# HGRN values of seven heads turned through memory and VectorE instead of TensorE, and the decode steps moved behind the heads' decode products, in a hybrid HGRN2 / Mamba-2 layer

## The chip, the cores and the metric

The kernel runs on one core of one Trainium2 chip. The metric is the device time of one launch, in microseconds. A core has five engines that take their instructions in order and wait for each other by semaphores: TensorE (PE in the profile, with its weight loads as PEld), VectorE (DVE), ScalarE (ACT), GpSimd (POOL) and SyncE (SP). In this kernel nearly all DMAs are issued by SP, in the order in which they stand in its queue; an issue that has to wait for something holds back every issue behind it.

## The reference

One decoder layer is computed for two groups of tokens: a prompt of 1024 tokens, and eight single tokens (decode) that bring recurrent states of their own. Per layer:

```
proj = rmsnorm(x) @ w_in                      # 1024 -> q, f, i, g, z, xbc, dt
# group A, HGRN2, 8 heads of 128 x 128
f = lb + (1-lb)*sigmoid(f_r);  k = 1-f;  q = silu(q_r);  v = i_r
S_t = f_t * S_(t-1) + k_t v_t^T;   o_t = q_t S_t        # chunks of 64
o_a = rmsnorm(o) * silu(g)
# group B, Mamba-2, 16 heads of 64, state 128
xbc = silu(conv(xbc));  h_t = exp(A dt_t) h_(t-1) + dt_t x_t B_t^T;  y_t = C_t h_t + D x_t
y = rmsnorm(y * silu(z))
x = x + concat(o_a, y) @ w_out
x = x + (silu(conv(gate)) * val) @ w_down      # gate, val = rmsnorm(x) @ w_up
```

After a final RMSNorm the two outputs and all new states are returned: among them the HGRN states of the prompt (`hgrn_prompt`) and of the eight decode tokens (`hgrn_sample`), and the SSM states of the decode tokens (`ssm_sample`).

## The kernel before, in words

Activations lie with the feature on the 128 partitions and the 1032 tokens (T = 1024 prompt tokens, then ND = 8 decode tokens, NT in all) along the free dimension. A matrix product of full precision is made of three products of halves (`hh` by `wh`, `hl` by `wh`, `hh` by `wl`): a weight tile `ws` comes from memory by DMA (512 KB), ACT rounds it to `wh` (L199), DVE makes the remainder `wl` (L201), and TensorE runs 72 matmuls over three column blocks of 344 tokens. One such job yields one of the arrays `f`, `q`, `v`, `sg` of one HGRN head, which ACT evicts from PSUM in three pieces (L924).

The program has, in order, the input projection and the SSM part (to about 370 us), eight HGRN heads (372.6 to about 870 us), and the output projection with the MLP. `head(h, t)` is a generator of small PE steps (score products `a`, state products `od` and `kv`, outputs `o`) with DVE, ACT and POOL work between them. TensorE's order is written out: `drive` interleaves the steps of head h with the four weight jobs of head h+1, so that TensorE has matmuls `mm<-hl,wh` to do while DVE works for the head. The orders of the other engines and of SP's queue are made by a scheduler from dependencies and estimated times; `tc.issue_after(x)` puts an instruction behind x in its engine's order.

What a head does, by the names of the profile:

- `vd<-ident,v` (L940) turns the eight decode columns of `v`; `vd` goes to memory (`vd_d`, L949) and comes back broadcast over the partitions as `vb`, two times 256 KB.
- `vtp<-ident,v` (L945), eight transposes on TensorE into two PSUM banks, and `vt<-vtp` (L946), two copies on ACT, give `vt`: the values with tokens on the partitions. `vt` is used by the products `kv<-vt,kt` and `o<-am,vt` some 40 us later.
- POOL and DVE update the decode states `Sh` (L958 to L960) with `vb`, `k` and `f`, and SP stores them (L961).
- The scores: DVE multiplies `k` and `q` by powers of `f` level by level in `scale` (L980, L981, with the running products `tt`, L986), and TensorE forms `a<-q,k`, `a<-v,k`, `a<-q,f`. The array `v` is overwritten by `v<-q,f` (L1009) as soon as `vtp` has read it.
- `od` (decode products from `Sh`) is copied to `odr` (L1051); `ktp` and `kt` turn the keys; `kv` gives chunk states, summed by DVE in `SS` (L1072, L1074); `o` gives the outputs; `hms` and the steps `nt` (L735 to L737) give the reciprocal norm, which goes to memory (`hr_d<-nt`, L1109) and comes back broadcast as `sq<-hr_d` (two times 256 KB). `sg<-sg,sq` (L1121) scales the head's output with it, and SP stores it (`mix_d<-sg`, L1122). These last steps run at the start of the next head.
- In heads 1 to 6 `decode_beside` does one of the SSM decode blocks beside the head, in three parts: `load` (DMAs of `Sd`, `Bb`, `Cb`, 1.5 MB in all, L690 to L693), `front` (ACT scales `Sd` eight times, L701; DVE forms `Bb` and `Sd`, L698 and L702; POOL multiplies `Cb`, L705) and `back` (two DVE reductions L710, and L711). After the last block of a group, `decode_gate` and `decode_norm` follow (`dg`, `xdk`; in heads 3 and 7).
- In the output part, `xs<-xb_d` tiles are turned by a VectorE transpose of 32 x 32 blocks (`xs<-xs`, L901). `xb_d` holds the prompt written in runs of 128 bytes in such an order that turning the blocks gives the whole transpose.

Of the kernel before, what the change touches and what calls it, by code (L numbers as in the profile page):

```python
# [8 lines left out]
F32 = mybir.dt.float32  # L9
# [15 lines left out]
H = 8  # L25
# [25 lines left out]
def hybrid_layer(  # L51
# [37 lines left out]
    def bank(s, tag="mx"):  # L89
        return psmx.tile([P, 512], F32, tag=tag, bufs=NBANK[tag], name=nm(s))  # L90
# [586 lines left out]
    def decode_beside(g, i):  # L677

        j = g * 4 + i
        xdd = small.tile([P, 2, ND], F32, tag="xdd", name=nm("xdd"))  # L680
        xdec = xdk[:, j, :]
        Sd, Bb = tl("e", "Sd")[:, :T], tl("e", "Bb")[:, :T]
        Cb = [tl("d", "Cb")[:, :512] for _ in range(2)]

        def d8(t):
            return t.rearrange("p (b n) -> p b n", n=P)

        def load(behind):
            with tc.issue_after(behind.ins):
                SP.dma_start(d8(Sd), state_ssm[0, :, 2 * j:2 * j + 2].rearrange("b h p n -> (h p) b n"))  # L690
# [24 lines left out]
        return load, front, back  # L715
# [16 lines left out]
    def rstd_of(dst, tmp, ps, n):  # L732

        A.activation(dst, ps, AF.Abs_reciprocal_sqrt, bias=epsc, scale=1.0 / n)
        V.scalar_tensor_tensor(tmp, ps, n * EPS, dst, op0=ALU.add, op1=ALU.mult)  # L735
        V.scalar_tensor_tensor(tmp, tmp, -0.5 / n, dst, op0=ALU.mult, op1=ALU.mult)
        V.scalar_tensor_tensor(dst, tmp, 1.5, dst, op0=ALU.add, op1=ALU.mult)  # L737

    gr_d = dram.tile([2, 4, 256], F32, name="gr_d")

# [83 lines left out]
    def once(work):  # L824
        def run():
# [22 lines left out]
    G.affine_select(eye8, eye8, pattern=[[1, ND], [-1, ND]], compare_op=ALU.is_equal, fill=0.0, base=0,  # L848
                    channel_multiplier=0)
    vd_d = dram.tile([H, ND, P], F32, name="vd_d")  # L850
    hr_d = dram.tile([H, 4, 256], F32, name="hr_d")

    am = const.tile([P, NC, P], F32, name="am")
# [58 lines left out]
    def head_in(h):  # L912
        t = {}

        def f_end():
            f, k = t["f"], tl("big" if h else "e", "k")
            A.activation(f[:, :NT], f[:, :NT], AF.Identity, bias=lbt2[:, 0, h:h + 1], scale=lbt2[:, 1, h:h + 1])
            V.tensor_scalar(k[:, :NT], f[:, :NT], -1.0, 1.0, op0=ALU.mult, op1=ALU.add)
            t["k"] = k

        for n, off, func in (("f", OFF_F, AF.Tanh), ("q", OFF_Q, AF.Silu), ("v", OFF_I, AF.Copy),
                             ("sg", OFF_G, AF.Silu)):
            def evict(c, cs, ps, n=n, func=func):
                A.activation(t[n][:, cs], ps, func, scale=0.5 if n == "f" else 1.0)  # L924

            def begin(n=n):
                t[n] = tl("e" if h == 0 and n == "f" else "big", n)

            if h == H - 1 and n == "sg":
                in_job_last(f"{n}{h}", off + h * P, evict, begin)  # L930
            else:
                in_job(f"{n}{h}", off + h * P, evict, begin, f_end if n == "f" else None)
        return t

    def head(h, t):
        f, k, q, v, sg = (t[n] for n in ("f", "k", "q", "v", "sg"))
        step_ = decode_beside((h + 1) // 4, (h + 1) % 4) if 1 <= h <= 6 else None

        dps = bank("vd", "nx")
        PE.transpose(dps[:ND, :P], v[:, T:NT], ident)  # L940
        vt = [half("vt"), half("vt")]
        for hf in range(2):
            ps = bank("vtp")
            for i in range(4):
                PE.transpose(ps[:, blk[i]], v[:, hf * 512 + i * P:hf * 512 + (i + 1) * P], ident)  # L945
            A.copy(vt[hf], ps)  # L946
# [5 lines left out]
        for b0 in (0, 4):  # L952
            bs = slice(b0, b0 + 4)
            ds = slice(T + b0, T + b0 + 4)
            Sd, vb = tl("ld", "Sh"), tl("d", "vb")[:, :512]
            fetch(d4(Sd), state_hgrn[0, bs, h].rearrange("b k v -> k b v"))
            fetch(vb, vd_d[h, bs].rearrange("b n -> (b n)").unsqueeze(0).to_broadcast([P, 512]))
            G.tensor_tensor(d4(vb), d4(vb), cb(k[:, ds]), op=ALU.mult)  # L958
            V.tensor_tensor(d4(Sd), d4(Sd), cb(f[:, ds]), op=ALU.mult)
            G.tensor_tensor(Sd, Sd, vb, op=ALU.add)  # L960
            kept_ = SP.dma_start(hgrn_sample[0, bs, h].rearrange("b k v -> k b v"), d4(Sd))  # L961
            Sds.append(d4(Sd))
        if step_:
            step_[0](kept_)

# [78 lines left out]
        turned_ = A.copy(am[0:64, :, 64:P], p6[0:64, :].rearrange("p (c t) -> p c t", t=64))  # L1044

        ops = bank("od", "nx")
        for b in range(ND):
            g = b % 4
            mm(ops[32 * g:32 * g + 32, :P], qb[:, b, :], Sds[b // 4][:, b % 4, :], start=(b < 4), stop=(b >= 4))
        odr = small.tile([P, P], F32, tag="odr", bufs=1, name=nm("odr"))  # L1050
        held = V.tensor_copy(odr, ops[:, :P])  # L1051
        if step_:
            step_[1](held, turned_)
        yield 3.5

        for hf in range(2):
# [22 lines left out]
        mm(dps[:, :ND], odr, selod)  # L1079
        od = small.tile([P, 3, ND], F32, tag="dsq", name=nm("od"))  # L1080
        held = V.tensor_copy(od[:, 0, :], dps[:, :ND])
        A.activation(od[:, 1, :], dps[:, :ND], AF.Square)
        yield 3.2
        if step_:
            step_[2](held)


        for hf in range(2):
# [16 lines left out]
        for g in range(4):  # L1105
            mm(ps[32 * g:32 * g + 32, :256], ones[:, 0:32], sq[g // 2][:, g % 2 * 256:g % 2 * 256 + 256])
        nt = half("nt")
        rstd_of(nt[:, 0:256], nt[:, 256:512], ps[:, :256], P)
        SP.dma_start(hr_d[h], nt[::32, 0:256])  # L1109

        oh = sg[:, T:NT]
# [507 lines left out]
```

## Time and profile before

| | |
|---|---|
| time, three runs | 1744.67 us median (1743.9 to 1748.21) |
| the profiled execution | 1747.35 us, of which the span from first to last instruction is 1745.6 us |
| TensorE clock granted | 0.996 of full speed |
| PE busy | 1704.6 us, 98% of the span |
| DVE, ACT, POOL busy | 1094.0, 782.0, 487.7 us (63%, 45%, 28%) |
| DMA | 200.22 MB in 250036 packets, 37.4% of the 16 engines' time on the main queue |

The device time is 1.75 us longer than the span in the profiled execution. An engine's busy time is an average over parts of the program with different limits, and a PE counted as busy runs matmuls back to back. A row of the timeline gives start, duration, engine, line, operation and operands, and in brackets the idle time before it with what ended it.

### The profile page before, as it was taken

Reading aid. Unit: us, or ns where it says so; the run is one execution under the profiler, and the core shown is the slowest. Engines: PE = TensorE matmul, PEld = TensorE weight load, DVE = VectorE, ACT = ScalarE, POOL = GpSimd, SP = SyncE. Lnnn points to the kernel's source line nnn. Section 1 sums busy time; section 2 is a strip of 40 time slices with the busy share of each in tenths; the row PEclk is TensorE's granted clock in tenths of the full one; section 3 lists DMA queues with packets and bytes.
Section 4 is the critical chain, followed back from the end, with each engine's and each line's share of the span. In section 5 each row is a group of like instructions: output and inputs, shape, how many; then the busy total and the mean of one; then the engine's idle time right before and its main releaser. Section 6 shows DMA issues by size and latency. Waiting matters only on the chain. (4 is left out here: it accounts for less than half of the span.)

```text
span 1745.6 us, 38507 instructions
## 1 busy us (share of the span) xinstructions
PE 1704.6 (98%) x16119; PEld 1657.3 (95%) x16119; DVE 1094.0 (63%) x1979; ACT 782.0 (45%) x1427; POOL 487.7 (28%) x501
## 2 busy tenths in 40 slices
PE   7999999999999999999999989999999999999998
PEld 7999999899989999999999989999999999999997
DVE  6668666555754655567746688666767667444545
ACT  7677685344445444445333464333334434111114
POOL 2102131110210211111122266666666664000002
PEclk9999999999999999999999999999999999999999
DMA  5354334533442443345437722222222226422212
GB/s 165 73 123 123 92 91 146 157 90 101 137 127 64 137 123 99 112 141 155 138 125 244 239 81 78 82 96 74 74 73 81 79 97 214 154 71 79 94 61 98
DMA packets 250036, 200.22 MB, mean 115 GB/s; under 512 B 47972, under 2 KB 221526, under 8 KB 249846
## 3 DMA queue, kind: packets, MB, share of 16 engines
q1 hardware_dynamic: 249574, 197.67, 37.4%
q8 instruction: 126, 2.06, 0.5%
q14 instruction: 48, 0.39, 0.1%
q0 software_dynamic: 288, 0.10, 0.0%
HBM read 155.16 MB, written 46.95 MB: 116 GB/s over the span
## 5 line engine op out<-in xcount | busy, mean ns | idle before, releaser
L93 PE MATMUL mm<-hl,wh 128*128 128x344 f32 x1248 | 405.2, 325 | 0.0
L93 PE MATMUL mm<-hh,wh 128*128 128x344 f32 x1248 | 404.9, 325 | 0.0
L93 PE MATMUL mm<-hh,wl 128*128 128x344 f32 x1248 | 402.0, 322 | 0.0
L93 PEld LDWEIGHTS mm<-hl,wh 128*128 128x128 f32 x1248 | 235.3, 189 | 4.8 <-issue 4.1
L93 PEld LDWEIGHTS mm<-hh,wh 128*128 128x128 f32 x1248 | 235.3, 189 | 4.0 <-issue 3.4
L93 PEld LDWEIGHTS mm<-hh,wl 128*128 128x128 f32 x1248 | 235.4, 189 | 1.4 <-issue 1.2
L199 ACT CAST wh<-ws 128x1024 fp32r<-128x1024 f32 x96 | 100.6, 1048 | 260.7 <-PE dn L93 134.8
L93 PE MATMUL ub<-uh,wh 128*128 128x258 f32 x704 | 200.1, 284 | 3.8 <-DVE fext L1432 2.7
L93 PE MATMUL ub<-ul,wh 128*128 128x258 f32 x704 | 199.5, 283 | 0.0
L93 PE MATMUL ub<-uh,wl 128*128 128x258 f32 x704 | 199.4, 283 | 0.0
L93 PE MATMUL dn<-ah,wh 128*128 128x256 f32 (+1 forms) x640 | 181.2, 283 | 2.0 <-DVE x L1549 2.0
L93 PE MATMUL dn<-al,wh 128*128 128x256 f32 (+1 forms) x640 | 180.6, 282 | 0.0
L93 PE MATMUL dn<-ah,wl 128*128 128x256 f32 (+1 forms) x640 | 180.1, 281 | 0.0
L201 DVE TENSOR_TENSOR wl<-ws,wh 128x1024 fp32r<-128x1024 f32 x88 | 109.7, 1247 | 93.3 <-ACT wh L199 92.6
L93 PE MATMUL mm<-mh,wh 128*128 128x258 f32 x512 | 146.5, 286 | 4.1 <-DVE x L1179 4.0
L93 PE MATMUL ua<-uh,wh 128*128 128x258 f32 x528 | 149.5, 283 | 0.8 <-DVE val L1444 0.4
L93 PE MATMUL ua<-ul,wh 128*128 128x258 f32 x528 | 149.2, 282 | 0.0
L93 PE MATMUL ua<-uh,wl 128*128 128x258 f32 x528 | 148.4, 281 | 0.0
L93 PE MATMUL mm<-ml,wh 128*128 128x258 f32 x512 | 145.3, 284 | 0.6 <-DVE ml L1136 0.6
L93 PE MATMUL mm<-mh,wl 128*128 128x258 f32 x512 | 144.9, 283 | 0.0
L93 PEld LDWEIGHTS ub<-uh,wh 128*128 128x128 f32 x704 | 133.6, 190 | 4.4 <-DVE fext L1432 2.9
L1382 DVE TENSOR_TENSOR wl<-wt,wh 128x512 fp32r<-128x512 f32 x88 | 89.4, 1035 | 74.2 <-ACT wh L1381 74.2
(373 smaller groups left out, 3987.4 us busy)
## 6 DMA issues: line engine op xcount, KB each, us to landing
ws<-in_w_in_dram SPq DMA_DIRECT2D x52, 512.0 KB
ws<-in_w_up_dram SPq DMA_DIRECT2D x44, 512.0 KB
ws<-in_w_out_dram SPq DMA_DIRECT2D x24, 512.0 KB
act_d<-val SPq DMA_DIRECT2D x22, 516.0 KB
al<-act_d SPq DMA_DIRECT2D x22, 516.0 KB
ws<-in_w_down_dram SPq DMA_DIRECT2D x22, 512.0 KB
ml<-mix_d SPq DMA_DIRECT2D x48, 172.0 KB
csb<-cs_d SPq DMA_DIRECT2D x32, 256.0 KB
```

Source lines behind the costliest of these rows:

```text
L93: PE.matmul(out, lhsT, rhs, start=start, stop=stop)
L199: A.copy(wh[:, :n], ws[:, :n])
L201: V.tensor_tensor(wl[:, :n], ws[:, :n], wh[:, :n].bitcast(F32), op=ALU.subtract)
L1382: V.tensor_tensor(lo[:, cs], sums[name], hi[:, cs].bitcast(F32), op=ALU.subtract)
```

## The change

Three things change inside `head` and `decode_beside`.

1. In heads 0 to 6 TensorE no longer turns `v`. When the last piece of `v` has been evicted (in the head before), SP writes it to a new array in memory, `vb_d`, in four DMAs of 128-byte runs (`v_end`, 512 KB per head). In the head, behind the second store of `Sh` in SP's queue, two DMAs read it back as `vt` (256 KB each), and DVE turns each by blocks of 32 x 32 (`V.transpose`), placed behind the copy of `odr`. Head 7 keeps TensorE's transposes.
2. `load` of the SSM decode block now depends on the last `od` matmul (`oded`) by a semaphore, where it used to stand behind the store of `Sh`. Its other three DMAs stand behind the first one.
3. `front` is ordered behind the copy and the square of `od` (`held`, `turned_`), and `back` behind the last step of `nt`.

The heart of the diff:

```
         def load(behind):
-            with tc.issue_after(behind.ins):
-                SP.dma_start(d8(Sd), state_ssm[0, :, 2 * j:2 * j + 2].rearrange("b h p n -> (h p) b n"))
+            first_ = SP.dma_start(d8(Sd), state_ssm[0, :, 2 * j:2 * j + 2].rearrange("b h p n -> (h p) b n"))
+            tc.add_manual_dep(first_.ins, behind.ins.name,
+                              mybir.DependencyInfo(mybir.DependencyClass.Sync, mybir.DependencyReason.DATA))
+            with tc.issue_after(first_.ins):
                 SP.dma_start(Bb, bc_d[2 * g].rearrange("b n -> (b n)").unsqueeze(0).to_broadcast([P, T]))
...
+    vb_d = dram.tile([H - 1, P, NC, P], F32, name="vb_d")
...
+        def v_end():
+            for b in range(4):
+                SP.dma_start(vb_d[h, :, :, 32 * b:32 * b + 32].rearrange("(a j) c r -> j c a r", j=32),
+                             t["v"][32 * b:32 * b + 32, :T].rearrange("j (c a r) -> j c a r", a=4, r=32))
...
         for hf in range(2):
+            if h < H - 1:
+                later_vt.append((vt[hf], vb_d[h, :, 4 * hf:4 * hf + 4, :]))
+                continue
             ps = bank("vtp")
...
-            kept_ = SP.dma_start(hgrn_sample[0, bs, h].rearrange("b k v -> k b v"), d4(Sd))
+            stored = SP.dma_start(hgrn_sample[0, bs, h].rearrange("b k v -> k b v"), d4(Sd))
             Sds.append(d4(Sd))
-        if step_:
-            step_[0](kept_)
+
+        for dst, src in later_vt:
+            with tc.issue_after(stored.ins):
+                SP.dma_start(dst.rearrange("p (c n) -> p c n", n=P), src)
...
+            oded = PE.matmul(ops[32 * g:32 * g + 32, :P], qb[:, b, :], Sds[b // 4][:, b % 4, :], start=(b < 4), stop=(b >= 4))
+        if step_:
+            step_[0](oded)
         odr = small.tile([P, P], F32, tag="odr", bufs=1, name=nm("odr"))
-        held = V.tensor_copy(odr, ops[:, :P])
-        if step_:
-            step_[1](held, turned_)
+        copied = V.tensor_copy(odr, ops[:, :P])
+        if h < H - 1:
+            for hf in range(2):
+                with tc.issue_after(copied.ins):
+                    V.transpose(vt[hf], vt[hf])
...
-        A.activation(od[:, 1, :], dps[:, :ND], AF.Square)
+        turned_ = A.activation(od[:, 1, :], dps[:, :ND], AF.Square)
+        if step_:
+            step_[1](held, turned_)
...
-        rstd_of(nt[:, 0:256], nt[:, 256:512], ps[:, :256], P)
+        held = rstd_of(nt[:, 0:256], nt[:, 256:512], ps[:, :256], P)
+        if step_:
+            step_[2](held)
```

TensorE's order loses the 56 transposes `vtp<-ident,v` of heads 0 to 6 and is otherwise the same, except that the product `dgs<-dg,ones` stands some matmuls later in its two places. The orders that the scheduler makes for DVE and SP change at more places than the diff names. Three of them follow; the numbers behind the names are buffers and differ between the two programs.

SP's queue at the change from head 4 to head 5, before. `hr_d` and `sq` carry the norm of head 4, `vd_d` and `vb` the decode values of head 5, `ws` weight tiles.

```order
L703 DMA out_dram<-Sd_7104 128x8x128
L1077 DMA out_dram<-SS_7706 128x128
L196 DMA ws_8176<-in_w_in_dram 128x8x128
L1109 DMA hr_d<-nt_7832 4x256
L182 DMA sq_7772<-hr_d 128x512
L182 DMA sq_7784<-hr_d 128x512
L949 DMA vd_d<-vd_7902 8x128
L196 DMA ws_8398<-in_w_in_dram 128x8x128
L182 DMA vb_7907<-vd_d 128x512
L182 DMA vb_7915<-vd_d 128x512
```

The same place of SP's queue after the change.

```order
L1096 DMA out_dram<-SS_7673 128x128
L926 DMA vb_d<-v_7593 256x4x32 x4
L1130 DMA hr_d<-nt_7814 4x256
L962 DMA vd_d<-vd_7875 8x128
L196 DMA ws_8147<-in_w_in_dram 128x8x128
L182 DMA sq_7754<-hr_d 128x512
L182 DMA sq_7766<-hr_d 128x512
L182 DMA vb_7880<-vd_d 128x512
L182 DMA vb_7888<-vd_d 128x512
L196 DMA ws_8361<-in_w_in_dram 128x8x128
```

The two loads `sq` stood ahead of `vd_d` and now stand behind it and behind one weight tile; heads 3, 4 and 6 read alike, and in head 1 they stand behind `vd_d`. The four stores `vb_d` are new.

DVE's order at the start of head 5, before. `sg<-sg,sq` finishes head 4; the steps on `k`, `v`, `f`, `q` and `tt` are the scores of head 5.

```order
L1009 TENSOR_TENSOR v_7626<-q_7403,f_7158 128x1024
L1121 TENSOR_TENSOR sg_6974<-sg_6974,sq_7772 128x512
L1121 TENSOR_TENSOR sg_6974<-sg_6974,sq_7784 128x512
L986 TENSOR_TENSOR tt_7926<-f_7158 128x512
L986 TENSOR_TENSOR tt_7927<-tt_7926 128x256
...
L980 TENSOR_TENSOR k_7394<-k_7394,f_7158 128x512
L981 TENSOR_TENSOR v_7626<-v_7626,f_7158 128x512
L1005 COPY_PREDICATED amc_7928<-mlow,a_929_7965 128x256
L980 TENSOR_TENSOR f_7158<-k_7394,tt_7926 128x256x2
L981 TENSOR_TENSOR q_7403<-v_7626,tt_7926 128x256x2
```

The same place of DVE's order after the change.

```order
L1024 TENSOR_TENSOR v_7593<-q_7378,f_7133 128x1024
L1142 TENSOR_TENSOR sg_6963<-sg_6963,sq_7754 128x512
L995 TENSOR_TENSOR k_7369<-k_7369,f_7133 128x512
L1142 TENSOR_TENSOR sg_6963<-sg_6963,sq_7766 128x512
L996 TENSOR_TENSOR v_7593<-v_7593,f_7133 128x512
L1001 TENSOR_TENSOR tt_7897<-f_7133 128x512
L995 TENSOR_TENSOR f_7133<-k_7369,tt_7897 128x256x2
L996 TENSOR_TENSOR q_7378<-v_7593,tt_7897 128x256x2
```

The small steps `tt`, `amc` moved behind `q<-v,tt`; the two `sg<-sg,sq` still stand ahead of it, the second one with only `v`, `tt` and `f` between.

SP's queue at the start of head 2 after the change. Before, head 2 had the order shown for head 5.

```order
L962 DMA vd_d<-vd_5496 8x128
L196 DMA ws_5781<-in_w_in_dram 128x8x128
L196 DMA ws_6001<-in_w_in_dram 128x8x128
L182 DMA vb_5501<-vd_d 128x512
L1130 DMA hr_d<-nt_5436 4x256
L182 DMA vb_5509<-vd_d 128x512
L182 DMA sq_5369<-hr_d 128x512
L182 DMA sq_5381<-hr_d 128x512
```

Here `hr_d` itself has moved behind `vd_d`: on DVE the steps `nt` of head 1 now stand behind `v<-q,f` of head 2, and `sg<-sg,sq` behind them.

DVE's order in head 7, before and after, from `k<-k,f` on; `dg` and `xdk` end the SSM decode.

```order
L980 TENSOR_TENSOR k_8952<-k_8952,f_8715 128x512
L736 SCALAR_TENSOR_TENSOR dg_9319<-dg_9319 128x8
L981 TENSOR_TENSOR v_9181<-v_9181,f_8715 128x512
L737 SCALAR_TENSOR_TENSOR dg_9319<-dg_9319 128x8
L1016 TENSOR_TENSOR amc_9474<-a_1081_9567,eyec 128x256
L730 SCALAR_TENSOR_TENSOR xdk<-xdk,vcol,dg_9319 128x8 x4
L980 TENSOR_TENSOR f_8715<-k_8952,tt_9472 128x256x2
L981 TENSOR_TENSOR q_8961<-v_9181,tt_9472 128x256x2
```

After the change the same stretch is shorter.

```order
L995 TENSOR_TENSOR k_8919<-k_8919,f_8682 128x512
L996 TENSOR_TENSOR v_9140<-v_9140,f_8682 128x512
L1031 TENSOR_TENSOR amc_9447<-a_1066_9529,eyec 128x256
L995 TENSOR_TENSOR f_8682<-k_8919,tt_9445 128x256x2
L996 TENSOR_TENSOR q_8928<-v_9140,tt_9445 128x256x2
```

The steps `dg` and `xdk` now stand behind `q<-v,tt`.

More of the change, by code (lines that the diff above doesn't have):

```diff
@@ L736, in rstd_of @@
         V.scalar_tensor_tensor(tmp, tmp, -0.5 / n, dst, op0=ALU.mult, op1=ALU.mult)
-        V.scalar_tensor_tensor(dst, tmp, 1.5, dst, op0=ALU.add, op1=ALU.mult)
+        return V.scalar_tensor_tensor(dst, tmp, 1.5, dst, op0=ALU.add, op1=ALU.mult)
     gr_d = dram.tile([2, 4, 256], F32, name="gr_d")
@@ L919, in f_end @@
             t["k"] = k
+        def v_end():
+            for b in range(4):
+                SP.dma_start(vb_d[h, :, :, 32 * b:32 * b + 32].rearrange("(a j) c r -> j c a r", j=32),
+                             t["v"][32 * b:32 * b + 32, :T].rearrange("j (c a r) -> j c a r", a=4, r=32))
+        ends = {"f": f_end, "v": v_end if h < H - 1 else None}
         for n, off, func in (("f", OFF_F, AF.Tanh), ("q", OFF_Q, AF.Silu), ("v", OFF_I, AF.Copy),
@@ L931, in head_in @@
             else:
-                in_job(f"{n}{h}", off + h * P, evict, begin, f_end if n == "f" else None)
+                in_job(f"{n}{h}", off + h * P, evict, begin, ends.get(n))
         return t
@@ L937, in head @@
         step_ = decode_beside((h + 1) // 4, (h + 1) % 4) if 1 <= h <= 6 else None
+        later_vt = []
         dps = bank("vd", "nx")
@@ L1043, in head @@
             A.copy(am[b:b + 32, :, b + 32:b + 64], c32(ps[:, :256])[b:b + 32])
-        turned_ = A.copy(am[0:64, :, 64:P], p6[0:64, :].rearrange("p (c t) -> p c t", t=64))
+        A.copy(am[0:64, :, 64:P], p6[0:64, :].rearrange("p (c t) -> p c t", t=64))
         ops = bank("od", "nx")
@@ L1048, in head @@
             g = b % 4
-            mm(ops[32 * g:32 * g + 32, :P], qb[:, b, :], Sds[b // 4][:, b % 4, :], start=(b < 4), stop=(b >= 4))
+            oded = PE.matmul(ops[32 * g:32 * g + 32, :P], qb[:, b, :], Sds[b // 4][:, b % 4, :], start=(b < 4), stop=(b >= 4))
+        if step_:
+            step_[0](oded)
         odr = small.tile([P, P], F32, tag="odr", bufs=1, name=nm("odr"))
-        held = V.tensor_copy(odr, ops[:, :P])
-        if step_:
-            step_[1](held, turned_)
+        copied = V.tensor_copy(odr, ops[:, :P])
[3 more added lines that the diff above has]
+                    V.transpose(vt[hf], vt[hf])
         yield 3.5
@@ L1081, in head @@
         held = V.tensor_copy(od[:, 0, :], dps[:, :ND])
-        A.activation(od[:, 1, :], dps[:, :ND], AF.Square)
+        turned_ = A.activation(od[:, 1, :], dps[:, :ND], AF.Square)
+        if step_:
+            step_[1](held, turned_)
         yield 3.2
-        if step_:
-            step_[2](held)
         for hf in range(2):
```

## The prediction

> **What bounds the kernel now.** I read the page's engine totals first, then the windows head by head, then what TensorE waited for, and only then the timeline at the places that the change touches. The totals:
>
> ```profile
> span 1745.6 us, 38507 instructions
> PE 1704.6 (98%) x16119; PEld 1657.3 (95%) x16119; DVE 1094.0 (63%) x1979; ACT 782.0 (45%) x1427; POOL 487.7 (28%) x501
> ```
>
> TensorE is busy 98% of the span; no other engine passes 63%. The windows of heads 3 and 5 (length; busy us and instructions of PE, PEld, DVE, ACT, POOL; granted clock, DMA share, GB/s) say whether that holds in the stage that is changed:
>
> ```profile
> 564.00:626.00 62.00, 62.00 (x827) 59.69 (x825) 37.16 (x72) 32.46 (x55) 9.01 (x6) 1.00 0.41 115
> 688.00:749.00 61.00, 61.00 (x816) 59.00 (x815) 35.20 (x63) 28.45 (x51) 8.87 (x6) 1.00 0.41 116
> ```
>
> In heads 3 and 5 PE has no gap at all (62.00 of 62.00, 61.00 of 61.00) with DMA at 0.41. So a matmul taken out of a head shortens the run, as long as no other engine becomes late by the same step. What PE did wait for, in total, count and longest:
>
> ```profile
> PE a L93 <- issue: 5.2, 3, 2.5
> PE a L93 <- DVE q L981: 2.3, 1, 2.3
> ```
>
> In the heads there are three waits of 5.2 us in which the profile shows no semaphore, and one wait for DVE, in head 7.
>
> **The transposes that go.** The start of head 5 on PE:
>
> ```profile
> 688.68 0.27 PE L940 MATMUL vd<-ident,v 128*8 128x128 f32 x1
> 688.79 1.03 PE L945 MATMUL vtp<-ident,v 128*128 128x128 f32 x8
> 689.58 0.40 PE L93 MATMUL mm<-hh,wh 128*128 128x344 f32 x1
> 689.82 0.32 PE L93 MATMUL mm<-hl,wh 128*128 128x344 f32 x1
> 689.98 0.32 PE L93 MATMUL mm<-hh,wl 128*128 128x344 f32 x1
> ```
>
> The durations overlap, so I use starts. From `vd` at 688.68 to the second `mm` at 689.82 are 1.14 us; `vd` alone takes the 0.11 us to the next row and an `mm` takes 0.16 (689.82 to 689.98), which leaves 0.87 us for eight transposes. Seven heads give 7 x 0.87 = **-6.1 us**. ACT also loses 14 copies `vt<-vtp`, but ACT is busy 28 to 32 us of these windows of 61 and 62, so they count nothing.
>
> **What replaces them.** DVE gets 14 block transposes. The same instruction on the same shape is in the trace, beside the copy behind which it is put and the product that needs it:
>
> ```profile
> L901 DVE STREAM_TRANSPOSE xs<-xs x16: 670/708/716, 839.0 to 918.5; 128x512 f32<-128x512 f32 x16
> L1051 DVE COPY odr<-od x8: 281/282/284, 408.5 to 842.5; 128x128 f32<-128x128 f32 x8
> L93 PE MATMUL kv<-vt,kt x128: 270/275/275, 414.1 to 847.8; 128*128 128x128 f32 x128
> ```
>
> Two take 1.4 us. From the start of `odr` to the first `kv` are 5.6 us in the first head (408.5 to 414.1) and 5.3 in the last; less 0.3 for the copy, at least 3.6 us remain, so this is hidden: 0. In memory it adds 512 KB written and 512 KB read per head. The write has the form of the `xb_d` stores (128-byte runs). Its DMAs start in the head before, ahead of the reads by the `Sh` updates, and no engine but SP waits for them; DMA stands at 0.41. I take 0.
>
> **The late norm.** This is the term that matters. In head 5 SP and DVE now run so:
>
> ```profile
> 685.10 0.52 SPq L1109 DMA_DIRECT2D hr_d<-nt  x1
> 686.78 0.82 SPq L182 DMA_DIRECT2D sq<-hr_d  x2
> 689.29 0.29 SPq L949 DMA_DIRECT2D vd_d<-vd  x1
> 691.05 0.40 SPq L196 DMA_DIRECT2D ws<-in_w_in_dram  x1
> 691.55 0.99 SPq L182 DMA_DIRECT2D vb<-vd_d  x2
> ...
> 690.95 1.22 DVE L1009 TENSOR_TENSOR v<-q,f 128x1024 f32<-128x1024 f32 x1
> 692.08 1.29 DVE L1121 TENSOR_TENSOR sg<-sg,sq 128x512 f32<-128x512 f32 x2
> 693.28 0.68 DVE L986 TENSOR_TENSOR tt<-f 128x512 f32<-128x512 f32 x1
> ...
> 697.11 1.20 DVE L980 TENSOR_TENSOR f<-k,tt 128x512 f32<-128x512 f32 x1
> 698.23 1.80 DVE L981 TENSOR_TENSOR q<-v,tt 128x512 f32<-128x512 f32 x1
> ...
> 696.64 1.12 POOL L958 TENSOR_TENSOR vb<-vb,k 128x512 f32<-128x512 f32 x1 [30.71 <-DMA vb<-vd_d]
> ...
> 701.75 0.75 PE L93 MATMUL a<-q,f 128*32 128x32 f32 x64
> ```
>
> I count from the head's first PE step, 688.68. `q<-v,tt` ends at +11.35 and `a<-q,f` wants it at +13.07; without the transposes it wants it at about **+12.2**. Now `sq` was issued 1.9 us before the head and was there when DVE came to it. After the change it is issued behind `vd_d` (+0.6) and one `ws`, so at about +1.4. When does it land? The row with the same shape is `vb`: 256 KB broadcast behind a 512 KB weight tile, issued 691.55, used by POOL at 696.64, 5.1 us. That gives +6.5 at the latest; if the weight tile is no hindrance it may be +4.5. From then DVE does `sg`, `k`, `sg`, `v`, `tt` at 0.6 us each (692.08 to 693.28 is two of them), then `f` 1.1 and `q` 1.8: 5.9 us, ending at +10.4 to +12.4. The steps that meet POOL are slower: `f` took 1.20 and `q` 1.80 while POOL ran, where `tt` of the same size took 0.68. POOL's work will now meet `sg`, `v` and `tt` as well, at up to 0.5 us each: up to +13.9. Against +12.2 that is a stall of 0 to 1.7 us a head; I take 0.5, nearer the low end since only the last-landing case reaches the high one. Five heads (1, 3, 4, 5, 6): **+2.5** (0 to +8.5).
>
> [...]
>
> Head 2 is worse. `hr_d` waits for `nt`, which now follows `v<-q,f` on DVE:
>
> ```profile
> 683.73 0.42 DVE L735 SCALAR_TENSOR_TENSOR nt<-hms,nt 128x256 f32<-128x256 f32 x1 [3.28 <-ACT nt L734]
> ```
>
> Three steps of this length take 1.3 us. `v<-q,f` ends at +3.5, so `hr_d` goes out at about +5.0 and `sq` 1.7 us later (685.10 to 686.78), +6.7. If it lands 2.5 us later DVE needs `sg`, `sg`, `tt`, `f`, `q`, at 0.6 each 3.0 us when POOL is done: +12.2, no stall; if it takes 5.1 and POOL still runs, +16.5, 4.3 us. I take **+2.7**.
>
> **Head 7.** Its wait for `q`:
>
> ```profile
> 817.15 1.71 DVE L980 TENSOR_TENSOR k<-k,f 128x512 f32<-128x512 f32 x1
> 818.78 1.00 DVE L736 SCALAR_TENSOR_TENSOR dg<-dg 128x8 f32<-128x8 f32 x1
> 819.71 0.68 DVE L981 TENSOR_TENSOR v<-v,f 128x512 f32<-128x512 f32 x1
> 820.31 1.25 DVE L737 SCALAR_TENSOR_TENSOR dg<-dg 128x8 f32<-128x8 f32 x1
> 821.82 0.63 DVE L730 SCALAR_TENSOR_TENSOR xdk<-xdk,vcol,dg 128x8 f32<-128x8 f32 x4
> 822.37 0.68 DVE L980 TENSOR_TENSOR f<-k,tt 128x512 f32<-128x512 f32 x1
> 823.80 0.44 PE L93 MATMUL a<-q,f 128*32 128x32 f32 x15 [2.33 <-DVE q L981]
> ```
>
> `dg` and `xdk` leave this stretch: 1.00 + 1.25 + 0.63 = 2.9 us. Some of their length was POOL's doing, which then falls on `f` and `q`. The wait was 2.33, so **-1.8** (0 to -2.3).
>
> **The decode loads.** `Sd`, `Bb` and `Cb`, 1.5 MB, leave the place behind the `Sh` stores for that behind `od`, some 18 us later in the rows of head 4, and the `Sd` steps go behind the square of `od`. DVE and ACT have room there (head 5):
>
> ```profile
> 640.12 1.15 SPq L690 DMA_DIRECT2D Sd<-in_state_ssm_dram  x1
> 658.01 0.65 PE L93 MATMUL od<-Sh,qb 128*32 128x128 f32 x16
> ...
> 734.64 1.22 DVE L201 TENSOR_TENSOR wl<-ws,wh 128x1024 fp32r<-128x1024 f32 x1 [1.76 <-ACT wh L199]
> 733.56 1.05 ACT L199 CAST wh<-ws 128x1024 fp32r<-128x1024 f32 x1 [3.22 <-PE mm L93]
> ```
>
> ACT sat idle 3.22 us before 733.56 and DVE 1.76 before 734.64, and in DVE's new order only the last `SS`, which no `o` needs, stands behind `Sd`. So 0; if the loads came late, the weight cast behind them would be held 1 to 2 us in each of six heads.
>
> The three waits called "issue" are left. From the page's DMA queues, and from head 4:
>
> ```profile
> q8 instruction: 126, 2.06, 0.5%
> ...
> 649.51 0.21 PE L93 MATMUL a<-v,k 128*16 128x16 f32 x2 [1.92 <-issue]
> ```
>
> The queue for instructions moves 16 KB a packet (2.06 MB by 126), by the same DMA engines. The wait in head 4 stands in the middle of a row of equal matmuls, 9.4 us after the decode loads were issued; I read it as instructions that came late behind those 1.5 MB. Those loads move away; but other bursts move toward other blocks (`vb_d`, and the loads in their new place). Worth between -5.2 and +5 (two new ones of the longest, 2.5); I take **-1.5**.
>
> [...]
>
> **Sum:** -6.1 + 2.5 + 2.7 - 1.8 + 0 - 1.5 = -4.2 us. The profiled execution took 1747.35 (span 1745.6 and 1.75 around it), so 1743.15. It lies 2.7 above the median of the runs; on that basis 1744.67 - 4.2 = 1740.5.
>
> **The rivals.**
>
> 1. *The late norm decides: slower.* If `sq` lands at +8.5 instead of +6.5 in heads 1 and 3 to 6, because `vb_d` and the weight tile share the queue, `q<-v,tt` ends near +15.2 and each head stalls 3 us: -6.1 + 5 x 3.0 + 4.3 - 1.8 = +11.4, **1756**. With these other terms the sign turns from a stall of 0.7 us a head, and 0.3% is passed from about 1.8. For it: the order is strict, and head 2 shows the case. Against it: DMA is at 0.41. Chance 0.17.
> 2. *New waits for instructions.* The three go, but as many come elsewhere: +5 in place of -1.5 gives +2.3, **1747**. Chance 0.14.
> 3. *All covers hold.* `sq` in time in the five heads, the "issue" waits gone, head 2 with 1: -6.1 + 1 - 2.3 - 5.2 = -12.6, **1732**. For it: the wait of head 4 behind the decode loads. Chance 0.22.
> 4. *The transposes were free*, the change does nothing: **1744.7**. PE at 62.00 of 62.00 speaks against it. Chance 0.03.
>
> **How the numbers follow.** My sum has chance 0.44; its terms spread it over about 1736 to 1744. 0.3% is 5.2 us, about what a measurement of this kernel can tell from no change, so the line lies at 1739.4, just under my value: of the 0.44 I give 0.18 to faster, 0.26 to same. With rival 3 faster is 0.40; same is 0.26 + 0.10 (most of rival 2) + 0.03 + 0.01 = 0.40; slower 0.16 + 0.04 = 0.20. The range, 1731 to 1753, leaves out the upper part of rival 1 and a tail below.
>
> **What would show it.** Right: 56 fewer PE instructions; windows of heads 3 to 6 about 60 us long with PE nearly full; a wait of `a` for `q` L996 in head 2 of 2 to 4 us and below 1 in the others; head 7's wait under 1. Wrong: `sg<-sg,sq` waiting for DMA beyond +7 in every head, `kv` waiting for `vt`, or "issue" waits over 5 us in sum.

## The result and the profile after

The changed kernel takes 1759.72 us (median of 6 runs, 1758.55 to 1764.46), the kernel before 1744.58 beside it (6 runs, 1743.31 to 1750.37): 1.0083 times as long, 95% interval 1.0066 to 1.0099, or 15.1 us more. I had forecast 1740.5 and a range up to 1753. The profiled execution of the changed kernel took 1762.72, 3.0 above its median; its span is 15.4 longer than that of the profile before.

The page's totals, and what TensorE waited for between 370 and 900 us (total, count, longest):

```profile
span 1761.0 us, 38453 instructions
PE 1706.2 (97%) x16063; PEld 1657.5 (94%) x16063; DVE 1104.4 (63%) x1993; ACT 774.4 (44%) x1413; POOL 483.9 (27%) x501
PE a L93 <- DVE q L996: 12.9, 6, 3.7
PE mm L93 <- DVE ml L1157: 2.1, 1, 2.1
PE mm L93 <- issue: 1.1, 1, 1.1
PE mm L93 <- ACT x L1198: 1.1, 1, 1.1
...
PE a L93 <- issue: 0.3, 1, 0.3
```

The 56 transposes are gone (16119 to 16063 instructions on PE), and so are most of the waits called "issue" (5.2 to 1.4). In their place PE waits for `q<-v,tt` in six heads, 12.9 us where it was 2.3 in one. (`ml` and `x` belong to the output projection, whose first products run beside head 7.) The windows of heads 3 and 5, cut from one head's first matmul to the next one's (length; busy us and instructions of PE, PEld, DVE, ACT, POOL; granted clock, DMA share, GB/s):

```profile
571.60:637.30 65.70, 62.01 (x814) 59.67 (x813) 37.19 (x74) 31.57 (x53) 8.46 (x6) 0.97 0.44 124
697.90:761.50 63.60, 61.34 (x805) 59.26 (x804) 37.58 (x65) 27.50 (x49) 9.22 (x6) 0.97 0.46 127
```

Before, these heads were 61.5 and 60.5 us long from start to start, and full. Now PE is idle 3.7 and 2.3 us in them, and the granted clock is 0.97 instead of 1.00. What ends the idle time in head 5 is seen in the timeline of SP, DVE, POOL and PE:

```profile
699.40 0.93 SPq L182 DMA_DIRECT2D sq<-hr_d  x2
...
704.22 0.69 DVE L1142 TENSOR_TENSOR sg<-sg,sq 128x512 f32<-128x512 f32 x1 [2.86 <-DMA sq<-hr_d]
...
706.03 1.53 DVE L996 TENSOR_TENSOR v<-v,f 128x512 f32<-128x512 f32 x1
707.48 1.78 DVE L1001 TENSOR_TENSOR tt<-f 128x512 f32<-128x512 f32 x1
709.29 1.41 DVE L995 TENSOR_TENSOR f<-k,tt 128x512 f32<-128x512 f32 x1
710.63 1.75 DVE L996 TENSOR_TENSOR q<-v,tt 128x512 f32<-128x512 f32 x1
...
705.93 1.08 POOL L971 TENSOR_TENSOR vb<-vb,k 128x512 f32<-128x512 f32 x1 [17.76 <-DMA vb<-vd_d]
...
710.24 1.59 POOL L973 TENSOR_TENSOR Sh<-Sh,vb 128x512 f32<-128x512 f32 x1
...
712.52 0.75 PE L93 MATMUL a<-q,f 128*32 128x32 f32 x64 [2.26 <-DVE q L996]
```

The head starts at 697.87. `sq` is used at +6.3, and DVE stood still 2.86 us for it. Then `v`, `tt`, `f` and `q` each meet one of POOL's four steps (the first and the last are shown): they take 1.4 to 1.8 us, where `sg` before them takes 0.69. `q` ends at +14.5 instead of +11.35.

The wait is not its only cost. The granted clock in stretches of 4 us behind it, and behind a wait of 3.1 us late in the SSM part, from 316 on (columns as in the windows above):

```profile
712.00:716.00 4.00, 3.48 (x76) 3.47 (x77) 4.00 (x10) 1.27 (x2) 0.00 (x0) 0.74 0.63 197
716.00:720.00 4.00, 4.00 (x23) 4.00 (x23) 3.16 (x8) 2.52 (x4) 0.00 (x0) 0.84 0.26 70
...
316.00:320.00 4.00, 1.31 (x6) 1.31 (x7) 3.10 (x6) 2.42 (x8) 0.08 (x1) 0.74 0.43 139
320.00:324.00 4.00, 4.00 (x16) 4.00 (x15) 4.00 (x7) 2.70 (x4) 1.25 (x1) 0.50 0.51 109
324.00:328.00 4.00, 4.00 (x25) 4.00 (x24) 1.93 (x5) 0.46 (x1) 1.29 (x1) 0.90 0.94 181
```

One minus the clock, times 4 us, is the time lost: (0.26 + 0.16) x 4 = 1.7 us after the wait of head 5, (0.26 + 0.50 + 0.10) x 4 = 3.4 us at 316. Summed in this way from 300 to 1100 us the profile after loses 11.9 us, the profile before 5.1.

So the 15.4 us between the two spans are, from the rows: transposes 7 x 0.8 (measured below), -5.6; waits for `q` 12.9 - 2.3, +10.6; `ml` and `x` in head 7, 2.1 + 1.1 - 0.6, +2.6; "issue" 1.4 - 5.2, -3.8; clock 11.9 - 5.1, +6.8. That is +10.6. Another 2.7 of waits arose before the first head, and about 2 us are left over in small waits.

By place, 6.1 of the 15.4 us lie before the first head, which starts at 378.7 instead of 372.6 (2.7 of waits and 3.4 of the clock). PE is 2.5 us late at 300 already, and the half clock begins by 319; the first instruction that stands otherwise in any engine's order is SP's first store `vb_d`, at 321.4. The profiles of the runs below, with and without the new stores, start their first head anywhere from 372.8 to 376.9. So I take these 6.1 us for chance. Heads 0 to 6 are 7.9 us longer (445.0 against 437.1), and what follows 1.3. But both profiles lie about as far above their medians (2.8 and 3.0 us), and the medians differ by 15.1. If the 6.1 are chance, then about 6 us of the difference between the medians stand in no row of this pair, and their cause stays open.

### The profile page after: what moved, and what is told of

It is laid out like the page before. It is cut to its first block, busy times and chain, and to the rows that moved or that the text cites. A ratio compares the mean times of both kernels' runs of the same rounds, so it can differ in the third digit from the quotient of the medians.

```text
span 1761.0 us, 38453 instructions
## 1 busy us (share of the span) xinstructions
PE 1706.2 (97%) x16063; PEld 1657.5 (94%) x16063; DVE 1104.4 (63%) x1993; ACT 774.4 (44%) x1413; POOL 483.9 (27%) x501
## 5 line engine op out<-in xcount | busy, mean ns | idle before, releaser
L201 DVE TENSOR_TENSOR wl<-ws,wh 128x1024 fp32r<-128x1024 f32 x88 | 116.0, 1318 | 85.1 <-ACT wh L199 83.8
```

Of the source, the lines that this page charges most:

```text
L201: V.tensor_tensor(wl[:, :n], ws[:, :n], wh[:, :n].bitcast(F32), op=ALU.subtract)
```

## The experiments

The theory to test was: the loss is a matter of order. The new DMAs and steps make `sq`, and with it `sg<-sg,sq`, late, DVE's scores then run beside POOL, and PE waits for `q`. The rivals: the traffic of `vb_d` and `vt` (1 MB a head) delays other transfers wherever they stand; the waits themselves are cheap and the granted clock is the cost; the decode steps carry the loss.

The times before on the same chips were 1746.01 (first four), 1748.08 (next four), 1748.25 and 1747.30 (last two pairs). Ratios are given with their interval; a thousandth is 1.75 us.

**The two parts apart.** First only the turning through memory, with `load`, `front` and `back` where they were:

```
 # the kernel before, plus
+vb_d, v_end, later_vt and the two V.transpose of the change
```

> The kernel before with only the first part of the change: values through memory and VectorE in seven heads; the decode loads and steps stay where they were. SP's order has hr_d, a weight tile and vd_d ahead of sq here too. Theory A (late norm): the part that brings the four stores vb_d is the part that moves sq, so the waits for q come with it, 1752 to 1764 us. Theory C (the moved decode loads and steps cost the time): 1738 to 1743 us, the transposes gone and nothing else.

Measured: 1757.36, 1.0063 [1.0048, 1.0079], in the range of theory A. Then only the decode steps:

```
 # the changed kernel, but
-        ends = {"f": f_end, "v": v_end if h < H - 1 else None}
+        ends = {"f": f_end, "v": None}
 # and vtp / vt by TensorE in all heads
```

> The changed kernel without its first part: TensorE transposes the values of all heads, vb_d is not written, vt is not read back; decode loads and steps are moved as in the change. SP's order has sq ahead of vd_d as before. Theory A (late norm): no wait for q in heads 1 to 6, the waits called issue in heads 2 and 4 gone with the loads: 1737 to 1745 us. Theory C (the decode moves cost the time): 1752 us or more.

Measured: 1748.83, 1.0013 [1.0001, 1.0024], between the two theories. In its profile PE has no wait at all in heads 1 to 6, and a new "issue" wait of 3.2 us in head 7. The sum of both ratios' parts, 1.0076, is about the whole 1.0083: the turning through memory carries the loss. But in the first of the two runs the longest wait of PE in the heads is another one than in the changed kernel:

```profile
PE cst L346 <- DMA rt<-in_state_conv_ffn_dram: 6.4, 1, 6.4
PE mm L93 <- ACT x L1195: 2.9, 1, 2.9
PE a L93 <- DVE q L995: 2.7, 1, 2.7
```

`rt` are convolution states of the MLP, and `cst` are the products that turn them in head 2. The wait for `q` is in head 2 too. In heads 3 to 6 of this run PE does not wait for `q`: DVE gets `sq` earlier, because SP issues it directly behind `vd_d`, with no weight tile between: `sg` comes at +4.5 there instead of +5.9 to +6.5, and `q` ends at +9.3 in head 4. Both `cst` and `q` come back below.

**The norm's place.** In the changed kernel, `sg<-sg,sq` is ordered behind `q<-v,tt`:

```
+                qmark[h] = turned_q            # q<-v,tt of the next head
...
+                    with tc.issue_after(qmark[h + 1].ins):
                         V.tensor_tensor(sg[:, hb[hf]], sg[:, hb[hf]], sq[hf], op=ALU.mult)
-        after(48, scale_out)
+        after(72, scale_out)
```

> The changed kernel with one edit: the two steps sg<-sg,sq that finish head h are emitted later and stand behind q<-v,tt of head h+1 in DVE's order; SP's queue is as in the changed kernel, so sq still lands late. Theory A (late norm: DVE stands at sg<-sg,sq until sq has landed, q<-v,tt behind it makes PE wait, and a wait of about 2.4 us or more also lowers the granted clock): the waits of a for q in heads 2 to 6 (12.9 us in sum in the profile) go, and the clock stays up in the heads, so 1738 to 1744 us. Theory B (the new transfers slow all loads, and sq is one victim among others): DVE and POOL wait for other loads, the waits only change their names, 1754 to 1760 us.

Measured: 1755.11, 1.0053 [1.0035, 1.0070]. By the time alone this is what the traffic rival expected. The profile shows the head-5 chain mended (head start 692.1):

```profile
699.71 0.69 DVE L998 TENSOR_TENSOR q<-v,tt 128x512 f32<-128x512 f32 x1
```

`q` ends at +8.3 and no head from 4 to 6 waits for it. That gives back 5 us of the 15; what theory A expected was all of it. In head 2 the wait for `q` is gone, but `cst` now waits 5.0 us for `rt`; and head 3 still waits 2.5 us for `q`.

**POOL's part.** The changed kernel with POOL's steps cut short; it leaves out the update of the decode states but for 4 of 512 columns:

```
-            G.tensor_tensor(d4(vb), d4(vb), cb(k[:, ds]), op=ALU.mult)
+            G.tensor_tensor(vb[:, 0:4], vb[:, 0:4], k[:, ds], op=ALU.mult)
...
-            G.tensor_tensor(Sd, Sd, vb, op=ALU.add)
+            G.tensor_tensor(Sd[:, 0:4], Sd[:, 0:4], vb[:, 0:4], op=ALU.add)
```

> The changed kernel with POOL's four state steps of each head (vb by k, Sh plus vb) done on 4 of 512 columns, so that hgrn_sample is not computed in full; loads, stores, DVE's and SP's orders at the head starts stay. It asks what of the waits for q is the late landing of sq and what is DVE being slowed by POOL. In the changed kernel v, tt, f, q took 1.5 to 1.8 us each beside POOL against 0.69 alone. Theory A1 (the slowing by POOL carries the waits in heads 4 to 6): q ends near +10.5 there, the waits of 0.9, 2.5 and 2.7 us go and one loss of clock with them, head 2 keeps about 2 us, head 3 its wait for dg: 1747 to 1753 us. Theory A2 (the landing of sq carries them): all waits stay, 1757 to 1762 us.

Measured: 1754.18, 1.0038 [1.0012, 1.0064], 1 us above the range of theory A1. In head 5 (start 689.8) `sq` is used as late as before, and the steps behind it are short:

```profile
696.42 0.69 DVE L1142 TENSOR_TENSOR sg<-sg,sq 128x512 f32<-128x512 f32 x1 [3.18 <-DMA sq<-hr_d]
698.24 0.69 DVE L996 TENSOR_TENSOR v<-v,f 128x512 f32<-128x512 f32 x1
...
700.17 0.69 DVE L996 TENSOR_TENSOR q<-v,tt 128x512 f32<-128x512 f32 x1
```

`sg` comes at +6.6 and `q` is nevertheless done at +11.1. Heads 4 to 6 have no wait for `q` (there are "issue" waits of 0.9 and 2.8 us in heads 5 and 6). So in heads 4 to 6 a late norm alone costs nothing; it costs because it pushes four steps of DVE into the time of POOL's four. Heads 2 and 3 are another matter: they wait 4.1 and 1.5 us for `q` here, with POOL's steps at 0.5 to 0.7 us each.

**SP's order, or the traffic.** The stores `vb_d` go to another queue. This also puts `sq` back ahead of `vd_d`, in all heads in the first run and in heads 2 and 3 in the second:

```
-                SP.dma_start(vb_d[h, :, :, 32 * b
+                G.dma_start(vb_d[h, :, :, 32 * b      # first run; A.dma_start in the second
```

> The changed kernel with the stores vb_d issued from POOL's queue. SP's order then has sq ahead of vd_d in all heads, with one weight tile between them and the loads vb, as in the kernel before. Theory A (order on SP): no wait for q above 1 us but in head 3, 1738 to 1747 us. Theory B (the traffic): 1754 to 1762 us. If POOL is held up by making the runs itself, its steps for Sh become late and od waits: then above 1760 us with a wait for Sh in the list.

Measured: 1757.49, 1.0062 [1.0047, 1.0077]. The time falls where the traffic rival expected it, but not for its reason. Heads 4 and 5, with the same bytes written and read, have no wait at all and are 59.7 and 59.8 us long; head 6 has no wait for `q`, but one of 2.2 us called "issue". The two longest waits in the heads are:

```profile
PE cst L346 <- DMA rt<-in_state_conv_ffn_dram: 4.5, 1, 4.5
PE a L93 <- DVE q L996: 3.2, 1, 3.2
```

Again `rt` in head 2 and `q` in head 3. By ACT's queue:

> The changed kernel with the four stores vb_d of each head issued from ACT's queue instead of SP's; the same bytes in the same runs move. SP's order then has sq ahead of vd_d in heads 1 to 4 and directly behind it, without a weight tile between, in heads 5 and 6. Theory A (late norm by the order on SP): waits for q under 1 us in heads 2 to 4, at most 1 us in 5 and 6: 1737 to 1745 us. Theory B (the traffic itself): 1754 to 1760 us, since the traffic is the same.

Measured: 1771.03, 1.0142 [1.0125, 1.0159], the slowest of all and outside both ranges. What PE waits for most in the heads, and ACT's timeline at the end of head 1:

```profile
PE cst L346 <- DVE od L737: 10.5, 2, 6.1
...
486.62 5.08 ACTq L926 DMA_DIRECT2D vb_d<-v  x4
491.80 1.09 ACT L1117 ACTIVATE sq<-o 128x512 f32<-128x512 f32 x2 [5.21 <-DMA vb_d<-v]
```

ACT spends 5.1 us on issuing four DMAs, and the squares of the output wait behind it. On DVE, `v<-q,f` waits 2.6 us here until the store `vb_d` has read `v`, and the steps of `od` stand behind `v<-q,f`; PE's `cst` waits 6.1 us for them at this place and 4.4 at the end of head 2. The run shows what ACT's queue costs and says little about the two theories.

**What a wait costs beside its length.** Into the kernel before, in heads 3 to 6, go idle DVE steps between `v` and `f`, first 8, then 14:

```
+            if lv == 0 and 3 <= h <= 6:
+                for _ in range(8):             # 14 in the second
+                    with tc.issue_after(low_.ins):
+                        padded.append(V.transpose(padt, padt))
```

> The kernel before with 8 idle block transposes (128 x 256) on DVE put between v and f in heads 3 to 6, to make a short wait of TensorE by hand: f ends about 1.2 us too late in four heads. With e8 it asks what a microsecond of waiting costs. Both theories: 1749 to 1753 us and a granted clock like before's (0.995 to 0.998).

> The same with 14 idle transposes: f ends about 3.3 us too late in four heads, four waits of 3.3 us. Theory D (a wait above some 2.4 us also halves the granted clock for 3.4 us or twice that, 1.7 to 3.4 us more a wait, as in the profile of the changed kernel): 1764 to 1774 us, granted clock 0.987 to 0.992. Without it: 13 us of waits, 1757 to 1760 us, clock as before.

Measured: 1753.22, 1.0030 [1.0011, 1.0049], and 1768.72, 1.0130 [1.0111, 1.0149]. PE's waits for the padded step are these, in the first and then in the second:

```profile
PE a L93 <- DVE f L986: 4.1, 4, 1.9
```

```profile
PE a L93 <- DVE f L986: 14.7, 4, 4.9
```

The second costs 22.7 us (0.0130 x 1748) for 14.7 us of waits. By the clock's rows its profile loses 11.9 us from 300 to 1100, 6.8 more than the profile before; waits called "issue" shrink by 3.4 in it, and 14.7 + 6.8 - 3.4 is 18.1 of the 18.7 by which its span is longer. In the four heads with the waits the clock loses 6.8 us, where the profile before loses none: 1.7, 0, 1.7 and 3.4 behind waits of 4.9, 3.1, 3.1 and 3.7. In the first run no such wait passes 1.9 us, these heads lose no clock, and 4.1 us of waits cost 5.2 (2 to 9 by the interval). So in sum the long waits bring a loss of clock of near half their length, though a single one of 3.1 us can bring none.

**The cause put together.** If the loss is made only of things that stand in each other's way in heads 2 and 3 and of the norm's place, then a kernel without these three must gain. It turns `v` through memory in heads 1, 4, 5 and 6 only and has `sg<-sg,sq` behind `q<-v,tt`:

```
+    VTM = (1, 4, 5, 6)
-        ends = {"f": f_end, "v": v_end if h < H - 1 else None}
+        ends = {"f": f_end, "v": v_end if h in VTM else None}
...  # likewise where vt is loaded and turned
```

> The changed kernel with its values turned through memory only in heads 1, 4, 5 and 6 (TensorE turns them in heads 0, 2, 3 and 7), and with sg<-sg,sq ordered behind q<-v,tt. The decode steps stand as in the changed kernel. Theory D (all that the turning through memory costs is where other work lands: the norm ahead of q<-v,tt, in head 2 the loads rt behind vt, in head 3 the steps dg; the transfers themselves cost nothing): no wait of a for q over 0.5 us in heads 1, 4, 5 and 6, no wait of cst for rt in head 2, four heads shorter by 0.87 us: 3.5 us below the decode steps alone (1.0013 of the kernel before), so 0.998 to 1.001, with the waits called issue as the spread. Theory B (the traffic of vb_d and vt delays other DMAs): the four heads keep 1 to 2.5 us each of new waits and the ratio is 1.002 to 1.005.

Measured: 1741.30 (12 runs, 1739.29 to 1744.08), **0.9964 [0.9952, 0.9976]**: faster than both kernels, and by more than expected. The profile is that of the fastest of the twelve; it has no loss of clock from 300 to 1100, and "issue" waits of 1.8 us where the profile before has 5.2. The theory says nothing of where those fall, so the part of the gain beyond the expectation is luck. Heads 3 and 5, and the longest of what PE waits for from 370 to 900, with its wait for `q`:

```profile
560.60:622.10 61.50, 61.50 (x823) 59.25 (x821) 37.71 (x72) 32.35 (x55) 9.29 (x6) 1.00 0.40 113
681.80:741.50 59.70, 59.70 (x805) 57.69 (x803) 35.38 (x65) 27.26 (x49) 9.02 (x6) 1.00 0.49 135
...
PE mm L93 <- issue: 1.1, 2, 0.8
...
PE a L93 <- DVE q L1000: 0.4, 1, 0.4
```

Head 5 turns through memory and is full at 59.7 us, against 60.5 before, with DMA at 0.49 instead of 0.40: the traffic costs nothing there, and eight transposes are worth 0.8 us. The same with the decode steps where the kernel before has them:

> As the run before, but with the decode steps (load, front, back) where the kernel before has them, so that the turning through memory in heads 1, 4, 5 and 6 and sg<-sg,sq behind q<-v,tt are the only changes to the kernel before. Theory D: 3.5 us below the kernel before, less or more by one wait called issue (2 us), so 0.997 to 0.9995, the four heads 59.5 to 60 us long. Theory B: 1.001 to 1.004, with waits of a or cst in those heads.

Measured: 1747.57, 0.9998 [0.9985, 1.0011], a gain of 0.4 us where 3.5 were expected. In its profile heads 0 to 6 are together 4.9 us shorter than in the profile before, but the first head starts 3.2 us later, and what follows the start of head 7 takes 1.8 more; no row says why. A wait of 2.6 us called "issue" stands in head 2, as in the kernel before (2.5), with a clock loss of 1.7 behind it; in the run before, with the decode loads moved, head 2 has no wait:

```profile
524.82 0.25 PE L93 MATMUL a<-v,k 128*16 128x16 f32 x10 [2.62 <-issue]
```

Last, heads 2 and 3 are added back to the faster kernel, one at a time:

```
+    VTM = (1, 2, 4, 5, 6)       # first run
+    VTM = (1, 3, 4, 5, 6)       # second run
```

> The kernel that turns the values through memory in heads 1, 4, 5 and 6 with sg<-sg,sq behind q<-v,tt (0.9964 of the kernel before), with head 2 added. In SP's order the loads rt of head 2 move behind the stores of Sh and the loads of vt. Theory D: cst waits for rt by 4 to 5 us, the clock that follows costs another 1.7 to 3.4, the eight transposes give 0.9 back: 5 to 7.5 us more, ratio 0.999 to 1.001. If instead head 2 costs nothing by itself: 0.9 us less, 0.996.

> The same kernel (heads 1, 4, 5 and 6, sg<-sg,sq behind q<-v,tt) with head 3 added. In DVE's order of head 3 the steps dg and xdk, of which dg waits for ACT, move ahead of f<-k,tt and q<-v,tt. Theory D: a waits for q by 2 to 3 us, the clock that follows costs up to 1.7, the transposes give 0.9 back: 1.5 to 4 us more, ratio 0.9972 to 0.9988. If head 3 costs nothing by itself: 0.9 us less, 0.996.

Measured: head 2 brings the ratio to 1.0026 [1.0014, 1.0038], head 3 to 0.9993 [0.9980, 1.0006]: 10.8 and 5.1 us more than 0.9964. SP in head 2 of the kernel before, then SP and PE in head 2 of the first:

```profile
498.20 0.34 SPq L182 DMA_DIRECT2D rt<-in_state_conv_ffn_dram  x1
...
508.07 3.22 SPq L961 DMA_DIRECT2D out_dram<-Sh  x2
```

```profile
511.65 3.52 SPq L978 DMA_DIRECT2D out_dram<-Sh  x2
515.23 0.98 SPq L983 DMA_DIRECT2D vt<-vb_d  x2
516.26 1.37 SPq L182 DMA_DIRECT2D rt<-in_state_conv_ffn_dram  x3
...
520.33 0.58 PE L346 MATMUL cst<-ident,rt 16*128 16x16 f32 x4 [6.27 <-DMA rt<-in_state_conv_ffn_dram]
```

The loads `vt` are tied to the stores of `Sh`, which wait for POOL; `rt` now stands behind both and is issued at 516.26, where in the kernel before the first of the three went out ahead of the stores. PE waits 6.27 us. The first 2.2 of these pass before `rt` is issued at all; the other 4.1 are its landing, beside DMA engines that are busy at 1.00 from 516 to 520. The traffic of `vt` may have a share in that part, which no run separates. DVE in head 3 of the kernel before, then of the second:

```profile
569.73 0.15 DVE L735 SCALAR_TENSOR_TENSOR dg<-dgs,dg 128x8 f32<-128x8 f32 x1
...
570.93 0.63 DVE L730 SCALAR_TENSOR_TENSOR xdk<-xdk,vcol,dg 128x8 f32<-128x8 f32 x4
```

```profile
567.32 0.69 DVE L1000 TENSOR_TENSOR v<-v,f 128x512 f32<-128x512 f32 x1
570.64 0.17 DVE L737 SCALAR_TENSOR_TENSOR dg<-dgs,dg 128x8 f32<-128x8 f32 x1 [2.63 <-ACT dg L736]
...
572.09 3.49 DVE L732 SCALAR_TENSOR_TENSOR xdk<-xdk,vcol,dg 128x8 f32<-128x8 f32 x4
575.51 0.68 DVE L1007 TENSOR_TENSOR tt<-f 128x512 f32<-128x512 f32 x1
```

In the kernel before, `dg` and `xdk` are done ahead of `k` and wait for nothing. Now `dg`, waiting 2.63 us for ACT, and `xdk` hold the scores of head 3 for 8 us, from `v` to `tt`. But PE waits only 1.1 us for `q` in this head, where 2 to 3 were expected, with no clock loss behind it, and 2.0 us more are called "issue". The head is 64.2 us long, 2.7 more than in the run with four heads.

So head 2 costs more than the 5 to 7.5 us expected. Head 3's 5.1 lie above 1.5 to 4, but the two intervals together leave 2 to 8, and its profile shows the 2.7.

The pieces nearly close. From 0.9964, head 2 adds 0.0062 and head 3 0.0029, which makes 1.0055; the kernel with all seven heads and `sg` behind `q` measured 1.0053. The norm's old place adds 0.0030 and leads to 1.0083. Each ratio has an interval of 0.0012 to 0.0017 either way, so that they meet this closely is luck, and head 0, which no run adds alone, is taken at nothing in it (62.5 us long in the run with seven heads, 62.1 in the one with four).

## Why the prediction was wrong

**The transposes, -6.1: right.** With no wait in the way head 5 is 0.8 us shorter in the run with four heads (-5.6 for seven), and in the changed kernel the head starts `vd` at 697.87, `mm` at 697.90.

**The late norm, +2.5 for heads 1, 3, 4, 5 and 6: the step that failed.** My landing time was right: +4.5 to +6.5 forecast, +6.3 seen. Head 1, where no weight tile stands ahead of `sq`, has no wait, as the order allowed. What was mis-sized is the work behind it. I gave `v`, `tt`, `f` and `q` 4.1 us and left their meeting with POOL to the upper end of the range; they took 6.35 (706.03 to 712.38). In heads 4, 5 and 6 the waits are 0.7, 2.3 and 2.5, where I took 0.5 each and 1.7 at most; with head 3's 3.7 the term came to 9.2 us of waits, above even its upper end of 8.5. I had kept the low end although the quoted row of `q` beside POOL showed 1.80. The run with POOL cut short shows the size: the four steps take 0.69 us each there, against 1.4 to 1.8 beside POOL's steps on all columns.

**Head 3, in the same term: a step that I left out.** I read SP's order of heads 3, 4 and 6 as like head 5's and did not look for what moved on DVE there. I saw `dg` leave the chain of head 7 and did not ask where it stood in head 3. There it waited for ACT and held `q` back: PE waits 3.7 us for `q` in this head of the changed kernel. The head added alone, with `sg` out of the way, costs 5.1 by the ratios and 2.7 in its profile.

**Head 2, +2.7: the size of the wait right, its price not.** PE waits 3.3 us for `q`, inside my 0 to 4.3, in part by luck, for `sq` went out at +8.4 and not at +6.7. But behind this wait stood a second one: `rt`, pushed behind `vt` on SP. It shows as a wait of 5.0 us once the wait for `q` is gone. I had listed the reads of `vt` and no one else's place behind them, and called them 0. I had also written that head 2 had the order shown for head 5 before the change; it had not, for a load `rt` stood between `vd_d` and the weight tile, and that load is the one that moved. Head 2 is worth 10.8 us in the run that adds it alone. That run's profiled span is 13.6 longer than that of the run with four heads: 8.3 of it in head 2, 3.6 in head 6 (an "issue" wait of 2.4 and a clock loss of 1.7 behind it), 2.0 before the first head. What lies outside head 2 stays unexplained.

**Head 7, -1.8:** the wait for `q` went from 2.3 to 0.5 as forecast, but `ml`, which stands on DVE behind the two `sg` that wait for `sq`, now makes PE wait 2.1 us, and ACT's `x` 1.1. Before, `ml` had made it wait 0.6, a row of the list of waits that I left out when I called `q` the one wait for DVE.

**Decode loads 0, "issue" waits -1.5:** 0 is right: with the decode steps moved alone no wait of PE stands in heads 1 to 6. The "issue" waits fell by 3.8, nearer my lower end. In the kernel with four heads the moving pays, 0.9964 against 0.9998 without it. Taken alone it gave 1.0013, with the new "issue" wait of 3.2 in head 7. Where such waits land after an edit I could not foretell, and no run shows what they wait for.

**The clock: a term that I put at nothing, without a reason.** It is 6.8 us of the profile's 15.4. Half of it, 3.4, lies before the first head, in the part that I take for chance; in heads 0 to 6 the loss is 6.8 us against 1.7 before. The profile before already showed a loss of 1.7 us behind each of its waits of 2.5 and 2.3 us in heads 2 and 7, which the prediction does not mention.

**The signs.** None of the three signs that I had named for being wrong came: `sq` was there by +5.9 to +6.5 in heads 3 to 6, `kv` never waited for `vt`, and the "issue" waits were 1.4. Those that failed were signs of being right: waits for `q` above 1 us in heads 3, 5 and 6, and windows of 65.7 and 63.6 us instead of about 60.

**Rival 1** named the right chain and the right side, at a chance of 0.17, with the wrong lever: `sq` did not land at +8.5; the time came from POOL, and from two waits that it did not have.

## What to carry to other kernels

When a load or a small step moves in an in-order queue, list what now stands behind it in every unit of the loop, not in one that looks typical: here the two heads that were not like the rest make, by the ratios, three quarters of the distance from 0.9964 to 1.0083. Where DVE has slack only because POOL begins later, delaying DVE can cost twice, the delay and the overlap: in head 5 here DVE stood 2.86 us for `sq`, and `v`, `tt`, `f` and `q` then took 6.35 us, where they took 2.6 with POOL cut short. A change whose parts work can be kept by leaving it out where it collides: four heads instead of seven, with `sg` behind `q`, turned +0.8% into -0.4%.

## What the hardware showed that I had not expected

A wait of PE of 2 to 5 us is in these runs often, but not always, followed by a stretch at half clock (0.50 granted from 520 to 524 us of the changed kernel, behind the wait of 3.3 us in head 2). The wait of head 5 in the changed kernel ends at 712.52. Behind it matmuls `mm` at first still start every 0.16 us; from about 713.9 to 717.2 they start every 0.28 or 0.29, and then every 0.16 again:

```profile
713.47 0.32 PE L93 MATMUL mm<-hl,wh 128*128 128x344 f32 x1
713.63 0.32 PE L93 MATMUL mm<-hh,wl 128*128 128x344 f32 x1
...
714.25 0.49 PE L93 MATMUL mm<-hh,wl 128*128 128x344 f32 x1
714.53 0.49 PE L93 MATMUL mm<-hh,wh 128*128 128x344 f32 x1
...
717.37 0.32 PE L93 MATMUL mm<-hl,wh 128*128 128x344 f32 x1
717.53 0.32 PE L93 MATMUL mm<-hh,wl 128*128 128x344 f32 x1
```

The loss comes in steps of about 1.7 us (two of them, 3.4, at 316). The wait of 2.26 us here cost 1.7, and the one of 2.46 us in head 6 of the same profile nothing. In the run with 14 idle steps a wait of 3.09 us in head 5 cost 1.7 and one of 3.08 in head 4 nothing. A wait of 2.8 us late in the SSM part cost nothing in the run with four heads, whose clock stays at 1.00. So the length of a wait does not decide by itself, and the 2.4 us that I had named as a limit in two expectations, an estimate of mine, is none. No run here shows the rule by which one wait is charged and another is not.
